# Eight block products against seven in one projection of a decoder layer, with the weights' sums made in DRAM by accumulating DMAs

## The chip, the core and the metric

The kernel runs on one core of one Trainium2 chip. A time is the device time of one execution in microseconds (us); the time of a kernel is the median of its runs.

## The reference

One decoder layer for 256 tokens of width 1024. `h @ w_in` feeds a pooling branch and an attention branch, `w_out` joins them, and a layer norm follows. Then comes the part that the change touches, cross-attention into 256 memory tokens, and after it a SwiGLU feed-forward and a last norm:

```python
def memory_cross_attention(h, mem, w_xq, w_xkv, w_xo):
    q = (h @ w_xq).reshape(B_, S_, XATTN_HEADS, XATTN_HEAD_DIM)
    kv = mem @ w_xkv
    k = kv[..., :D].reshape(B_, M, XATTN_HEADS, XATTN_HEAD_DIM)
    v = kv[..., D:].reshape(B_, M, XATTN_HEADS, XATTN_HEAD_DIM)
    ...
```

The memory's values are `mem @ w_xkv[:, D:]`: 256 x 1024 times 1024 x 1024, float32.

## The kernel before

**Precision.** Every float32 operand is split into a high part (ScalarE casts it to fp32r, L170, L429) and a low part (VectorE subtracts the high part, L172, L430). A product is three matmuls into one PSUM bank: high by high, high by low, low by high (`three`, L359 to L364).

**Weights.** `Stream` (L50 to L203) holds all weight tiles of 512 KB in the order in which they are used. `fetch` (L89) issues a tile's load on SyncE's queue (L102) into one of 7 raw buffers; `fetch_ahead` (L112) issues as many as the raw buffers allow, and `before` (L81) hangs other loads in front of a tile's. `prepare` (L148) makes the high and the low part of the next tile, in one of 8 buffers. A stage that reads weights through `get` (L181) lets one more tile be prepared at each call, until the stream is 8 tiles ahead of the last one that is used up; `next` (L176) does the same once for each tile that is used up. `held` stops both.

**Order.** The order on each engine is the order of the program's text (`manual_schedule`, L219): generators give out a few matmuls at a time (`run`, L420), and what stands between two calls of `run` stands between those matmuls in every queue. An engine goes through its queue strictly in that order.

**The stages that matter here**, in TensorE's order:

- `do_u` (L620): two halves; after each, VectorE adds `upad` (L627) and GpSimd computes the windows' sums (`windows`, L590: L596, L599).
- `do_xk` (L641), the memory's keys. Between its products stand `mix_pool` (L605 to L611), a matmul for each pooling group. Its input is made by `pool_diff` (L601 to L603) on VectorE from the windows' sums.
- `project(c_mix, ...)` and norm 1 (L784 to L790), which gives `h1`.
- `do_xv` (L796): the memory's values, 4 pieces (token half by column half) with 8 row blocks each, 3 matmuls of 512 columns for each: 96 matmuls. Each weight tile is one row block, 128 x 1024, and serves four pieces. After 8 steps, four groups of four transposes of `h1` (L440, `transpose_tok`) stand between its products; each takes a bank of the pool `pmisc`, which has four, and `split` reads it into `h1T`. At the end each piece is split into high and low from PSUM (L801).
- `do_xq` (L815): the queries of four heads. The first takes its two banks from `pmisc`, the others from `pacc`. `xscores(0)` (L828) follows after 7 steps of the second head and needs the first head's queries, which ScalarE (L822) and VectorE (L823, L825) take out of PSUM.

PSUM has eight banks: four in `pacc` (`accbank`), four in `pmisc` (`bank`).

Of the kernel before, what the change touches and what calls it, by code (L numbers as in the profile page):

```python
# [206 lines left out]
def decoder_layer(  # L207
    ctx: ExitStack, tc: tile.TileContext, x, x_t, mem_t, w_qkv, w_u, w_pool, w_out,
    ln1_g, ln1_b, w_xq, w_xk, w_xkv, w_xo, ln2_g, ln2_b, w_gu, w_down, ln3_g, ln3_b, out,
):  # L210
# [28 lines left out]
    def rows(w, k0, c0, nk=1, width=D):  # L239
        return ws.add(w[k0 * P:(k0 + nk) * P, c0:c0 + width].rearrange("(k p) n -> p k n", p=P), 1)  # L240
# [110 lines left out]

    mhalf = cp.tile([P, 32], F32, name="mhalf")[:, 0:1]
    nc.vector.memset(mhalf, -0.5)
# [81 lines left out]

    def transpose_tok(dst, tok, t, k0):

        ps = bank("tp")
        for k in range(4):
            nc.tensor.transpose(ps[:, k * P:(k + 1) * P], tok[:, (k0 + k) * P:(k0 + k + 1) * P], ident)  # L440
        ts = slice(t * P, (t + 1) * P)
        split(*dst.parts(k0, 4, ts), ps.rearrange("p (k t) -> p k t", k=4))
# [170 lines left out]
    def do_v():  # L613
# [3 lines left out]
        for piece in pieces:  # L617
            nc.scalar.copy(vt[:, piece[0], :], acc[piece])

    def do_u():  # L620
        for c in range(2):
            pss = [accbank("pu") for _ in range(2)]
            yield from proj_both(pss, c_u[c], xT, 4)
            for f, ps in enumerate(pss):
                y = upad[:, 2 * c + f, PADW:]
                nc.scalar.copy(y, ps[:, S:])
                nc.vector.tensor_add(y, ps[:, :S], y)  # L627
            windows(c)

    xkT = (a8("xkTh", F32R), a8("xkTl", F32R))  # L630
# [148 lines left out]


    load_norm("g", 1, ln1_g)()
    load_norm("b", 1, ln1_b)()
    h1 = ap.tile([P, T, D], F32, tag="a8", name="h1")
    mix = project(c_mix, lambda k: (cT[0][:, k], cT[1][:, k]), 4)  # L784
    for t in range(T):
# [10 lines left out]
    def do_xv():  # L796
        acc = {piece: accbank("xv") for piece in PIECES}
        yield from proj_rows(acc, c_xv, mT.pair,
                             PIECES, True, True, True)
        for t, c0, c1 in PIECES:  # L800
            split(xv[0][:, t, c0:c1], xv[1][:, t, c0:c1], acc[t, c0, c1])  # L801

    gv = do_xv()
    run(gv, 8)
    for t in range(T):
        for k0 in (0, 4):
            transpose_tok(h1T, h1[:, t, :], t, k0)
            run(gv, 2)
    run(gv)


# [323 lines left out]
    for half in HALVES:  # L1135
# [30 lines left out]
_INS = ["x", "x_t", "mem_t", "w_qkv", "w_u", "w_pool", "w_out", "ln1_g", "ln1_b", "w_xq", "w_xk",  # L1166
        "w_xkv", "w_xo", "ln2_g", "ln2_b", "w_gu", "w_down", "ln3_g", "ln3_b"]

# [43 lines left out]
```

## Time and profile before

| | us |
|---|---|
| median of 3 runs | 376.72 (376.57 to 377.14) |
| the profiled execution | 376.66 |
| its span in the trace | 374.9 |
| TensorE busy | 368.5 (98%) |
| VectorE busy | 306.8 (82%) |
| ScalarE busy | 204.1 (54%) |
| GpSimd busy | 19.6 (5%) |
| DMA, mean | 192 GB/s |

In the rows below, PE is TensorE, PEld its weight loads, DVE VectorE, ACT ScalarE, POOL GpSimd, SP SyncE. A row of a timeline has the start, the busy time, the engine and line, the operation, output and inputs, shapes, the count, and in brackets how long the engine was idle before and what ended that. A row of the table by stretches has the length of the stretch, the busy time of each engine in it, the clock that TensorE was granted, the share of the time that the 16 DMA engines were busy, and GB/s.

### The profile page before, as it was taken

How to read it: one execution, taken by the hardware profiler on the slowest of the kernel's cores; microseconds unless marked ns; L12 is line 12 of the kernel's file. 1: busy time of each engine (PE TensorE's matmuls, PEld its weight loads, DVE VectorE, ACT ScalarE, POOL GpSimd, SP SyncE). 2: the span in 40 equal slices, each digit the busy share in tenths (PEclk: the TensorE clock that was granted, in tenths of full speed). 3: DMA queues.
4: the chain of work that ended last, by engine and by line, in shares of the span. 5: the costliest groups of instructions: out<-in, count | busy, mean ns of one | idle time of the engine just before them, and what ended most of it. 6: DMA issues, size and time to landing. Idle time of an engine off the chain costs nothing.

```text
span 374.9 us, 5582 instructions
## 1 busy us (share of the span) xinstructions
PE 368.5 (98%) x2061; PEld 317.6 (85%) x2061; DVE 306.8 (82%) x498; ACT 204.1 (54%) x330; POOL 19.6 (5%) x27
## 2 busy tenths in 40 slices
PE   9999999999999999999999999999999999999994
PEld 8997878787888889998888888888898888888883
DVE  6768799975599677865889688888888999999984
ACT  6746677644154635644237675567665675546510
POOL 1000033400020000000100000000000000000021
PEclk9999999999999999999999999999999999999998
DMA  8997784668508963343106958665554453375202
GB/s 274 415 416 270 222 282 124 214 214 292 169 0 281 387 210 133 113 156 123 60 2 221 326 184 278 226 219 176 173 180 170 152 170 113 119 275 162 64 0 112
DMA packets 20891, 71.93 MB, mean 192 GB/s; under 512 B 2304, under 2 KB 3072, under 8 KB 20736
## 3 DMA queue, kind: packets, MB, share of 16 engines
q1 hardware_dynamic: 20432, 71.12, 54.3%
q10 hardware_dynamic: 432, 0.46, 0.4%
q8 instruction: 16, 0.26, 0.3%
q14 instruction: 11, 0.09, 0.1%
HBM read 70.52 MB, written 1.05 MB: 191 GB/s over the span
## 4 chain that ended last, share of the span: by engine, by line
PE 97%; DMA 1%; DVE 1%; ACT 0%; issue 0%; POOLq 0%; ACTq 0%
PE pg L377 19%; PE pg L383 10%; PE pqk L483 6%; PE m L362 5%; PE m L364 5%; PE m L363 5%; PE acc L362 4%; PE acc L363 4%; PE acc L364 4%; PE pxk L377 4%; PE pxq L377 4%; PE pxq L383 2%; PE pu L377 2%; PE pxk L383 2%; PE xv L362 2%; PE xv L364 2%
## 5 line engine op out<-in xcount | busy, mean ns | idle before, releaser
L725 POOL TENSOR_TENSOR rs<-rs,mhalf 128x1 f32<-128x1 f32 x6 | 5.0, 830 | 291.2 <-DVE rs L724 291.2
L429 ACT CAST g<-sg 128x512 fp32r<-128x512 f32 x14 | 8.7, 621 | 19.1 <-DVE sg L983 12.4
L430 DVE TENSOR_TENSOR g<-sg,g 128x512 fp32r<-128x512 f32 x14 | 9.7, 692 | 8.9 <-ACT g L429 8.9
L964 DVE TENSOR_TENSOR sg<-pg,sg 128x256 f32<-128x256 f32 x40 | 14.1, 416 | 0.0
L963 ACT COPY sg<-pg 128x256 f32<-128x256 f32 x40 | 11.8, 379 | 2.1 <-PE pg L383 2.1
L968 ACT ACTIVATE sg<-sg 128x512 f32<-128x512 f32 x10 | 6.3, 635 | 12.1 <-DVE sg L964 12.0
L520 ACT ACTIVATE xpr<-xs,mx 128x256 f32<-128x256 f32 x8 | 3.7, 470 | 14.3 <-DVE mx L531 14.3
L520 ACT ACTIVATE pr<-pr,mx 128x128 f32<-128x128 f32 (+1 forms) x16 | 7.1, 445 | 7.6 <-DVE mx L551 7.6
L429 ACT CAST h2T<-tp 128x512 fp32r<-128x512 f32 x4 | 2.3, 586 | 12.9 <-PE tp L440 12.9
L730 DVE SCALAR_TENSOR_TENSOR r<-r,mv,gb 128x512 f32<-128x512 f32 (+2 forms) x12 | 8.3, 722 | 0.0
L717 DVE BATCH_NORM_STATS2 st<-r 128x6 f32<-128x512 f32 (+1 forms) x12 | 8.0, 670 | 0.3
L969 DVE TENSOR_TENSOR sg<-sg 128x512 f32<-128x512 f32 x10 | 6.9, 692 | 0.8
L596 POOL TENSOR_TENSOR win<-upad 128x542 f32<-128x542 f32 x2 | 4.0, 1998 | 56.9 <-DVE upad L627 56.9
L525 DVE RECIPROCAL sm<-sm 128x2 f32<-128x2 f32 x12 | 2.0, 166 | 6.0 <-ACT xpr L520 4.5
L835 PE MATMUL xs<-xkTh,xq 128*128 128x256 f32 x32 | 6.4, 282 | 0.0
L429 ACT CAST h1T<-tp 128x512 fp32r<-128x512 f32 x4 | 2.4, 588 | 7.2 <-PE tp L440 7.2
L735 DVE SCALAR_TENSOR_TENSOR h<-r,rs,gb 128x512 f32<-128x512 f32 x8 | 5.7, 746 | 0.1
L596 POOL TENSOR_TENSOR win<-win 128x269 f32<-128x269 f32 (+3 forms) x4 | 5.8, 1446 | 0.2
L635 ACT CAST xkTh<-pxk 128x256 fp32r<-128x256 f32 x8 | 2.6, 377 | 5.5 <-PE pxk L383 5.5
L637 DVE TENSOR_TENSOR xkl<-pxk,xkTh 128x256 f32<-128x256 f32 x8 | 3.0, 416 | 3.1 <-ACT xkTh L635 3.1
L835 PEld LDWEIGHTS xs<-xkTh,xq 128*128 128x128 f32 x32 | 5.2, 190 | 0.2
L170 ACT CAST w39h<-w39r 128x1024 fp32r<-128x1024 f32 x1 | 1.0, 1049 | 7.8 <-PE acc L364 7.8
(1157 smaller groups left out, 1294.8 us busy)
## 6 DMA issues: line engine op xcount, KB each, us to landing
gb<-in_ln_g SPq DMA_DIRECT2D x3, 512.0 KB, 6.0
gb<-in_ln_b SPq DMA_DIRECT2D x3, 512.0 KB, 7.5
wr<-in_w_qkv SPq DMA_DIRECT2D x5, 256.0 KB, 4.4
mr<-in_mem_t SPq DMA_DIRECT2D x1, 1024.0 KB, 11.4
xt<-in_x SPq DMA_DIRECT2D x1, 1024.0 KB, 7.8
xr<-in_x_t SPq DMA_DIRECT2D x3, 256.0 KB, 6.1
wr<-in_w_qkv SPq DMA_DIRECT2D x1, 512.0 KB, 6.0
w7r<-in_w_qkv SPq DMA_DIRECT2D x1, 512.0 KB, 6.9
```

The lines of the kernel that those rows point to most:

```text
L362: nc.tensor.matmul(ps, wa, ya, start=start, stop=False, skip_group_check=part)
L363: nc.tensor.matmul(ps, wa, yb, start=False, stop=False, skip_group_check=part)
L364: nc.tensor.matmul(ps, wb, ya, start=False, stop=stop, skip_group_check=part)
L377: nc.tensor.matmul(ps, hi[:, b * P:(b + 1) * P], yT.both(k), start=k == 0, stop=False, skip_group_check=True)
L383: nc.tensor.matmul(ps[:, S:], lo[:, b * P:(b + 1) * P], yT.pair(k)[0], start=False, stop=k == KD - 1, skip_group_check=True)
L429: nc.scalar.copy(h, ps)
L483: nc.tensor.matmul(qk[i][:, f, :], w[:, c * P:(c + 1) * P], y, start=k == 0 and f == 0 and w is hi and y is x_hi, stop=k == KD - 1 and w i ...
L520: nc.scalar.activation(dst[:, j, :], src[:, j, :], AF.Exp, bias=mx[:, j:j + 1], scale=sign, accum_out=sm[:, j:j + 1])
L596: nc.gpsimd.tensor_add(nxt[:, j:, 2 * n - 1:], cur[:, j:, 2 * n - 1:], cur[:, j:, n - 1:PADW + S - n])
L835: nc.tensor.matmul(ps[:, t, :], q[:, kk, t * P:(t + 1) * P], k[:, 2 * h + kk], start=n == 0, stop=q is q_lo and kk == 1, skip_group_check= ...
L963: nc.scalar.copy(y[:, f, :], ps[:, S:])
L964: nc.vector.tensor_add(y[:, f, :], ps[:, :S], y[:, f, :])
```

## The change

The memory's values are computed by a form of Strassen's and Winograd's scheme: both factors are cut into quarters (the memory by token half and by even and odd row block, the weights by even and odd row block and by column half), and seven products of quarters, each over 4 row blocks, replace eight. `z` holds two sums of two quarters of the weights, `w` a sum of three and a sum of all four. They are made in DRAM: SyncE copies quarters of the weights into two DRAM tensors of 2 MB (`xv_z`, `xv_w`), and GpSimd issues three accumulating DMAs (`add_quarters`): 2 MB into `xv_z`, then 2 MB from `xv_z` into `xv_w`, then 1 MB into one half of `xv_w`. The first stands after the first `windows`, the second before the second `windows`, the third behind it. The stream then holds 14 tiles of 512 KB for the values in place of 8: 4 of `y` (two quarters as they are), 2 of `o`, 4 of `z`, 4 of `w`; each serves two steps of 3 matmuls, and `o` too. VectorE makes four sums of the memory's quarters and splits them. The seven products have seven banks, all four of `pmisc` and three of `pacc`; the four groups of transposes share the eighth, `tp`. `keep_xv` combines the seven into the four pieces.

```diff
-    c_xv = [rows(w_xkv, k, D) for k in range(KD)]
+    dram = ctx.enter_context(tc.tile_pool(name="dram", bufs=1, space=bass.MemoryType.DRAM))
+    xv_z, xv_w = [dram.tile([P, 2, KD // 2, 512], F32, name=name) for name in ("xv_z", "xv_w")]
+    c_xv = {("y", j): ws.add(w_xv[:, 0:2, j, :], 1)[0] for j in range(KD // 2)}
+    c_xv |= {("o", j): ws.add(w_xv[:, 3, j:j + 2, :], 1)[0] for j in range(0, KD // 2, 2)}
+    c_xv |= {("z", j): ws.add(xv_z[:, :, j, :], 1)[0] for j in range(KD // 2)}
+    c_xv |= {("w", j): ws.add(xv_w[:, :, j, :], 1)[0] for j in range(KD // 2)}
...
+    ws.before(c_xk[2][0], lambda: nc.sync.dma_start(xv_z, w_xv[:, 1:3]))
+    ws.before(c_xk[3][0], lambda: nc.sync.dma_start(xv_w, w_xv[:, 0:2]))
...
-    def transpose_tok(dst, tok, t, k0):
-
-        ps = bank("tp")
+    def transpose_tok(dst, tok, t, k0, ps=None):
+
+        ps = bank("tp") if ps is None else ps
...
+    def add_quarters(step):
+
+        if step == 0:
+            nc.gpsimd.dma_start(xv_z, w_xv[:, 2:4], accum_op=OP.add, max_dma_last_dim=8192)
+        elif step == 1:
+            nc.gpsimd.dma_start(xv_w, xv_z[:, 1:2].to_broadcast([P, 2, KD // 2, 512]), accum_op=OP.add, max_dma_last_dim=8192)
+        else:
+            nc.gpsimd.dma_start(xv_w[:, 0], w_xv[:, 1], accum_op=OP.add, max_dma_last_dim=8192)
+
     def do_u():
         for c in range(2):
...
+            if c:
+                add_quarters(1)
             windows(c)
+            add_quarters(2 if c else 0)
...
+    m_parts = [[late.tile([P, 2, KD // 2, P], F32R, tag=part, name=f"ms{i}{part}") for part in ("hi", "lo")]
+               for i in range(2)]
...
+    nc.vector.tensor_sub(s1, a21, a22)
+    nc.vector.tensor_sub(s3, a11, a21)
+    nc.vector.tensor_sub(s2, s1, a11)
+    nc.vector.tensor_add(s4, a12, s2)
+    for i, y in enumerate(sums):
+        hi, lo = m_parts[i // 2]
+        split(hi[:, i % 2], lo[:, i % 2], y)
...
     def do_xv():
-        acc = {piece: accbank("xv") for piece in PIECES}
-        yield from proj_rows(acc, c_xv, mT.pair,
-                             PIECES, True, True, True)
-        for t, c0, c1 in PIECES:
-            split(xv[0][:, t, c0:c1], xv[1][:, t, c0:c1], acc[t, c0, c1])
-
-    gv = do_xv()
-    run(gv, 8)
+        v = {n: bank(f"v{n}") for n in (2, 3, 7, 5)}
+        v |= {n: accbank(f"v{n}") for n in (1, 4, 6)}
+        plan = {"y": ((2, "12"), (3, "s4")), "z": ((7, "s3"), (5, "s1")), "w": ((4, "22"), (6, "s2")),
+                "o": ((1, "11"), (1, "11"))}
+        counts = dict.fromkeys(v, 0)
+        for (what, j), number in c_xv.items():
+            ws.prepare(number + 1)
+            hi, lo = ws.tiles[number]
+            for half, (n, form) in enumerate(plan[what]):
+                counts[n] += 1
+                three(v[n], memory(form, j + half if what == "o" else j), (hi[:, half], lo[:, half]),
+                      counts[n] == 1, counts[n] == KD // 2, True)
+                yield
+            ws.used += 1
+            ws.next()
+        return v
+
+    def keep_xv(v):
...
+        nc.scalar.copy(v1, v[1])
+        nc.vector.tensor_add(c11, v[2], v1)
+        nc.scalar.copy(v5, v[5])
+        nc.vector.tensor_add(c12, v[3], v5)
+        nc.vector.tensor_add(u2, v[6], v1)
+        nc.vector.tensor_add(c21, v[7], u2)
+        nc.vector.tensor_sub(c12, c12, u2)
+        nc.vector.tensor_sub(v5, v5, c21)
+        nc.vector.tensor_add(c21, v[4], c21)
+        for i, y in enumerate((c11, c12, c21, v5)):
+            split(quarter(0, *divmod(i, 2)), quarter(1, *divmod(i, 2)), y)
...
+    run(gv, 7)
+    tp = accbank("tp")
     for t in range(T):
         for k0 in (0, 4):
-            transpose_tok(h1T, h1[:, t, :], t, k0)
+            transpose_tok(h1T, h1[:, t, :], t, k0, tp)
             run(gv, 2)
     run(gv)
+    keep_xv(values[0])
```

The host lays the weights out as quarters (`w_xv`), without arithmetic on them, and the buffer for descriptors of GpSimd's DMAs grows (`dynamic_dma_scratch_size` 256 to 1024).

More of the change, by code (lines that the diff above doesn't have):

```diff
@@ L778, in until, with memory @@
                 return got
+    mix = project(c_mix, lambda k: (cT[0][:, k], cT[1][:, k]), 4)
+    run(mix, 2)
+    m_parts = [[late.tile([P, 2, KD // 2, P], F32R, tag=part, name=f"ms{i}{part}") for part in ("hi", "lo")]
+               for i in range(2)]
+    quarter = mr[0].rearrange("p (j e) (t s) -> p e t j s", e=2, t=T)
+    a11, a21, a12, a22 = [quarter[:, e, t] for e in range(2) for t in range(T)]
+    sums = [sp.tile([P, KD // 2, P], F32, name="ms", tag="pr", bufs=PR_BUFS) for _ in range(4)]
+    s1, s3, s2, s4 = sums
+    nc.vector.tensor_sub(s1, a21, a22)
[5 more added lines that the diff above has]
+        split(hi[:, i % 2], lo[:, i % 2], y)
+    def memory(form, j):
+        if form in ("11", "12", "22"):
+            e, t = {"11": (0, 0), "12": (1, 0), "22": (1, 1)}[form]
+            return mT.pair(2 * j + e, slice(t * P, (t + 1) * P))
+        i, n = divmod(("s1", "s3", "s2", "s4").index(form), 2)
+        return tuple(part[:, n, j] for part in m_parts[i])
     load_norm("g", 1, ln1_g)()
@@ L1201 @@
     given["w_xq"] = chunks(given["w_xq"])
+    quarters = given["w_xkv"][:, D:].reshape(KD // 2, 2, P, 2, 512)
+    given["w_xv"] = np.stack([quarters[:, i, :, j].transpose(1, 0, 2) for i, j in ((1, 0), (1, 1), (0, 1), (0, 0))],
+                             axis=1)
     given["w_gu"] = np.concatenate([chunks(given["w_gate"]), chunks(given["w_up"])], axis=3)
```

18 lines of the change are left out of this document (13 added, 5 removed).

## The prediction

> **What bounds the kernel now.** I read the page's busy times first, then the waits of TensorE alone, then stretches of 10 us around the stage, then single engines' timelines there.
>
> ```profile
> PE 368.5 (98%) x2061; PEld 317.6 (85%) x2061; DVE 306.8 (82%) x498; ACT 204.1 (54%) x330; POOL 19.6 (5%) x27
> ...
> PE end L1156 <- ACT diag L1153: 1.5, 1, 1.5
> PE busy L453 <- PEq L1175: 0.8, 1, 0.8
> PE acc L362 <- DVE xkTl L639: 0.2, 1, 0.2
> ...
> 30.00:40.00 10.00, 10.00 (x48) 7.78 (x48) 8.78 (x33) 7.99 (x21) 0.00 (x0) 1.00 0.49 180
> ...
> 50.00:60.00 10.00, 10.00 (x63) 8.24 (x62) 9.43 (x25) 8.00 (x19) 3.09 (x4) 1.00 0.45 152
> 60.00:70.00 10.00, 10.00 (x63) 8.34 (x61) 9.72 (x17) 5.80 (x10) 7.51 (x6) 1.00 0.73 221
> ...
> 90.00:100.00 10.00, 10.00 (x46) 8.29 (x45) 5.06 (x5) 3.14 (x3) 0.00 (x0) 1.00 0.63 218
> ...
> 110.00:120.00 10.00, 10.00 (x48) 8.26 (x47) 10.00 (x12) 4.08 (x5) 0.00 (x0) 1.00 0.59 197
> ```
>
> TensorE is the bound: three waits in the whole span, 2.5 us together, and full in every stretch quoted. So each matmul removed is worth its slot, and each wait put in front of TensorE is lost in full, since no idle time is left to take it up. The second thing to see is VectorE: in 110 to 120, in the middle of the stage that is changed, it is busy for 10.00 of 10.00 us. It is no bound there, because its weight tiles are ahead of need; but more work on it, or a wait of TensorE on work that stands late in its queue, is not hidden. I make the sum against the profiled execution, 376.66 us, which is 0.06 below the median of the runs.
>
> **The gain: 12 matmuls.** The values take 84 matmuls in place of 96 (seven products of 4 blocks of 3, for eight).
>
> ```profile
> 106.46 0.39 PE L362 MATMUL xv<-w35h,mT 128*128 128x512 f32 x1
> ...
> 130.20 1.98 PE L377 MATMUL pxq<-h1T,w43h 128*128 128x512 f32 x8
> ...
> 117.51 0.44 PE tp L440 x4
> ```
>
> From the first of the values' matmuls to the first of the queries' it is 23.74 us. Four groups of transposes lie in it, 0.44 each by the chain of work. (23.74 - 1.76) / 96 = 0.229 us for a slot; 12 slots are **-2.75 us**. A step of three takes 0.69.
>
> **First cost: GpSimd waits between its two windows.** The built program's queue on GpSimd reads: first windows, first accumulating DMA, second accumulating DMA, second windows. The second DMA reads what the first has written and so waits for its landing; the second windows stand behind that wait. An issuing queue does stand still at a DMA whose condition isn't met:
>
> ```profile
> SPq L102 <- DVE w63l L172: 17.8, 1, 17.8
> ...
> 55.43 0.28 POOL L599 TENSOR_TENSOR win<-win,fac 128x16 f32<-128x16 f32 x1
> 62.18 2.00 POOL L596 TENSOR_TENSOR win<-upad 128x542 f32<-128x542 f32 x1 [6.46 <-DVE upad L627]
> ...
> 68.83 0.22 POOL L599 TENSOR_TENSOR win<-win,fac 128x16 f32<-128x16 f32 x1
> ...
> 69.09 0.94 DVE L603 SCALAR_TENSOR_TENSOR upad<-win,upad 128x256 f32<-128x256 f32 x1 [0.28 <-POOL win L599]
> ...
> 70.17 0.67 PE L607 MATMUL pm<-upad,pool_w 128*128 128x256 f32 x2
> ```
>
> GpSimd is done with the first windows at 55.71 and starts the second at 62.18, so the transfer has 6.47 us. Behind it everything is tight: the third group's sum ends at 69.05, VectorE's difference waits for it and ends at 70.03, TensorE's pooling matmul starts at 70.17. A delay above some 0.2 us goes through to TensorE, and VectorE's next weight tile queues behind the same difference.
>
> No row shows an accumulating DMA, so its 2 MB (2.10 million bytes) are bounded by loads.
>
> ```profile
> GB/s 274 415 416 270 222 282 124 214 214 292 169 0 281 387 210 133 113 156 123 60 2 221 326 184 278 226 219 176 173 180 170 152 170 113 119 275 162 64 0 112
> ...
> w30r<-in_w_out SPq DMA_DIRECT2D x1, 512.0 KB, 3.4
> ```
>
> At the fullest slices the engines move 416 GB/s: 512 KB are 1.26 us of it, so 2.1 of the 3.4 us that such a load takes are fixed. One pass over 2.10 MB is 5.05, landing after 7.2 us. A transfer that reads two sources is two passes if reading sets the pace, 12.2 us; if the write counts as well, three, 17.3 us. I take two passes. The other loads hold the engines for 0.45 and 0.73 of 50 to 70, and the two copies of 2 MB that SyncE issues before two key tiles push some of 40 to 50 into it; fair sharing with them makes 12.2 into something between that and 25. I take 15, nearer the lower end, since the weight loads there are ahead of their use and come in bursts. Landing at 55.71 + 15 = 70.7, the second windows start 8.5 late, TensorE loses **+8.3 us** (bounds: 0.5 from one pass undisturbed, 20 from a crowded two passes; less than nothing is excluded, as a wait on a full TensorE gives nothing back).
>
> [...]
>
> **Second cost: one bank for four groups of transposes.** Before, each group had its own bank; now they share `tp`, which VectorE frees when it has subtracted (the low part of `h1T`).
>
> ```profile
> 111.35 1.22 DVE L172 TENSOR_TENSOR w39l<-w39r,w39h 128x1024 fp32r<-128x1024 f32 x1
> 112.49 1.22 DVE L172 TENSOR_TENSOR w40l<-w40r,w40h 128x1024 fp32r<-128x1024 f32 x1
> ...
> L430 DVE TENSOR_TENSOR h1T<-tp,h1T 128x512 fp32r<-128x512 f32 x4 | 2.8, 691 | 2.8 <-ACT h1T L429 2.8
> L429 ACT CAST h1T<-tp 128x512 fp32r<-128x512 f32 x4 | 2.4, 588 | 7.2 <-PE tp L440 7.2
> ```
>
> A weight tile's low part takes VectorE 1.14 from start to start. It comes out of norm 1 at 111.35, then by the built order makes tiles 39, 40, 41 and only then the first `h1T`: 111.35 + 3 x 1.14 + 0.69 = 115.45. TensorE has the first transposes at 106.46 + 7 x 0.69 = 111.3 and wants the bank again two steps later, at 113.1: 2.3 lost. From there each round is 0.44 + 1.37 on TensorE and 1.14 + 0.69 on VectorE, nearly equal, 0.3 more in the other two. **+2.6 us**; the values end at 130.3 (106.46 + 84 x 0.229 + 1.76 + 2.8 with small change), no earlier than before.
>
> **Third cost: the banks that the first queries need.** Four banks of `pmisc` hold products until `keep_xv`. The first queries take the first two, which VectorE frees with its first two sums, and these stand behind tiles 45 to 52. After the fourth `h1T` (121.4, three rounds of some 1.97 behind the first) eight tiles are 9.1 us: 130.7 with the little idle between. The two sums, 0.65 each (between 0.69 from PSUM, above, and 0.6 from SBUF, below), free the banks at 131.35 and 132.0; TensorE wants both from 130.3 on, the second one matmul later: **+1.5 us**.
>
> ```profile
> 130.34 2.48 DVE L430 TENSOR_TENSOR xv<-xv,xv 128x512 fp32r<-128x512 f32 x4
> ...
> 87.31 0.33 SPq L102 DMA_DIRECT2D w41r<-in_w_xkv  x1
> ```
>
> The first of these rows gives the 0.6 (2.48 / 4); the second is used below.
>
> **Fourth cost: the first scores.** The stream no longer stands 8 tiles ahead when the queries begin: `next` lets one tile follow for each used up, so depth stays at 4, where `get` filled it at the start of the stage. The rest is made up in the first queries: in the built order tiles 53 to 58 stand in front of the first queries' low parts, on VectorE and on ScalarE. Before, three tiles did, and it was done in time:
>
> ```profile
> 137.32 0.42 DVE L823 SCALAR_TENSOR_TENSOR xql<-pxq,xq 128x256 f32<-128x256 f32 x1
> ...
> 138.56 0.42 DVE L825 SCALAR_TENSOR_TENSOR xq<-pxq,xql 128x256 fp32r<-128x256 f32 x1
> ...
> 138.94 0.28 PE L835 MATMUL xs<-xkTh,xq 128*128 128x256 f32 x1
> ...
> 139.10 1.43 PE xs L835 x12
> ```
>
> After: `keep_xv` is 7 sums of 0.65 and 4 low parts of 0.6 from 130.7, so 137.6; six tiles, 144.4; the queries' low parts take 1.66 as before (137.32 to 138.98), 146.1. TensorE needs 8.74 from the first query matmul to the scores (130.20 to 138.94), so is there at 131.8 + 8.74 = 140.6; a third of the scores needs the low parts, 0.48 at the end. It ends at 146.6 and not at 140.6 + 1.43 = 142.0: **+4.6 us**. After that VectorE's order is the old one, six tile numbers on; 0.3 more at the second scores are left out.
>
> **Costed at nothing.** The four sums of the memory's quarters and their splits (5 us of VectorE) stand ahead of tile 35, in 87 to 98, where VectorE is busy for 5.06 of 10 us; without that cover they would be in front of norm 1, 1:1. The six more loads (3 MB) fall where DMA engines are idle or tiles are ahead. The `z` tiles wait on SyncE for the first transfer, with norm 1's scale and shift behind them in that queue, the `w` tiles for the third; before, the load in the place of the first `z` tile was issued at 87.31, and by the estimates the transfers have landed by then (70.7, then some 15 and 9 more with the windows between); at twice these times SyncE would stand and the load of `w` would be late, which is in the upper end.
>
> **Sum.** 376.66 - 2.75 + 8.3 + 2.6 + 1.5 + 4.6 = **390.9 us**. The last three terms (8.7) come from queue orders and durations that rows show; the first cost is the wide one.
>
> **Rivals.**
>
> - *The transfer is cheap.* One pass, little company: landing at 62.9 to 66, term 0.5 to 3.5, so 383.1 to 386.1. For it: 0.49 of the DMA's time is in use in 30 to 40 and loads alone land in 3.4. Against: two copies of 2 MB stand ahead in the same engines. 0.22.
> - *The transfer is crowded.* If copies in DRAM run at less than a load's rate, they still occupy the engines at 55.7, and the term passes 15: 397.6 and more. 0.20.
> - *Faster.* The place is VectorE's queue from 111 on, the price its three terms. If TensorE isn't held there, because the tiles' low parts come out sooner than by the sum (the handing back of `tp` needs them 2.3 us sooner, the scores 4.6), and the transfer lands inside its 6.47 us, 373.9 remains. It decides where all waits together stay under 2.75. Against: VectorE is full in 110 to 120 already. 0.06.
> - *The clock.* In the stretches quoted the granted clock is 1.00, and TensorE never waits for over 1.5 us, so no row shows what a wait of 8 us does to the matmuls behind it. If the next seven took twice their 0.229, 1.6 would be lost: 392.5. I give that 0.4 where the first term is over 3.4; it stays inside the ranges of those cases and is not in the sum. [...]
>
> That fewer matmuls aren't made is excluded: the built order holds 84.
>
> **How the numbers follow.** The forecast's case (term 3.5 to 15, 386.1 to 397.6) has 0.50, cheap 0.22, crowded 0.20, faster 0.06, no change 0.02. What a measurement of this kernel can tell from no change is about 0.2%, 0.75 us. The range takes in the cheap case with a third of VectorE's terms not coming (380) and the crowded case to a term of 20 (403); beyond it are the faster case and the worst of the crowded.
>
> **What would show it.** After, GpSimd's second windows start near 71 and not at 62; TensorE waits before the pooling matmul of the third group, before the second transposes of `h1`, before the first query matmuls, and before the last part of the first scores. Wrong would be: the second windows at 62 to 63 (first term gone), or a values' stage of 21 us with the scores straight after (the other terms gone).

## The result and the profile after

The changed kernel takes 399.25 us (median of five runs, 397.56 to 399.85); the kernel before took 376.76 us beside it. The ratio is 1.0585, 95% interval 1.0558 to 1.0611: slower by 22.5 us. The forecast was slower, at 390.9 us with a range of 380 to 403. The ratios here and below leave out an execution that lies more than 1.5% above the fastest of its kernel; there is one such in three of the kernels below (394.11, 391.88 and 384.94 us), and only their medians take it in.

The profiled execution took 399.48 us with a span of 397.7 (before: 376.66 and 374.9). From its page, the busy times, the row of the granted clock in 40 slices, and the two accumulating DMAs with the time from issue to landing at the end of the line:

```profile
PE 375.5 (94%) x2049; PEld 322.1 (81%) x2049; DVE 323.1 (81%) x519; ACT 212.9 (54%) x342; POOL 19.7 (5%) x30
...
PEclk9999999679999889699999999999999999999998
...
xv_z<-in_w_xv POOLq DMA_DIRECT2D x1, 2048.0 KB, 17.4
xv_w<-xv_z POOLq DMA_DIRECT2D x1, 2048.0 KB, 17.0
```

TensorE makes 12 matmuls fewer and is busy for 7 us longer. That alone says that part of the loss isn't waiting: the same matmuls take longer. The row of the clock says where: 6 and 7 in the eighth and ninth slice, 8, 8, 9 and 6 in slices 14 to 17. Before, every digit but the last was 9.

TensorE's waits (total, times, longest):

```profile
PE pm L614 <- DVE upad L610: 9.2, 1, 9.2
PE tp L447 <- DVE h1T L437: 2.1, 1, 2.1
PE xs L919 <- DVE xq L909: 1.8, 2, 1.6
PE pxq L384 <- ACT v L870: 1.6, 1, 1.6
...
PE xs L919 <- ACT xq L906: 0.7, 1, 0.7
PE pxq L384 <- DVE c L869: 0.4, 1, 0.4
```

These are the four places that the prediction names, and no other: the third pooling matmul, the second transposes, the first queries, the first scores. (Of the last, 0.7 us are ahead of the scores, for their high parts; the prediction has only the wait for the low parts.) GpSimd's timeline shows the first of them at its source (start, length, then in brackets the idle time and what ended it):

```profile
55.85 1.33 POOL L630 DMA_DIRECT2D xv_z<-in_w_xv  x1
73.62 1.07 POOL L632 DMA_DIRECT2D xv_w<-xv_z  x1 [16.43 <-DMA xv_z<-in_w_xv]
74.23 1.57 POOL L603 TENSOR_TENSOR win<-upad 128x542 f32<-128x542 f32 x1
...
90.90 0.87 POOL L634 DMA_DIRECT2D xv_w<-in_w_xv  x1 [11.44 <-DMA xv_w<-xv_z]
```

The second windows begin at 74.23 and not at 62.18, behind the wait of the second DMA for the first.

Stretches of 2 us (the columns: length, then busy time and count of each engine, the granted clock, the share of the DMA engines, GB/s) show what follows each stop:

```profile
80.00:82.00 2.00, 2.00 (x9) 1.82 (x8) 1.61 (x4) 0.47 (x1) 0.00 (x0) 0.50 1.10 236
...
84.00:86.00 2.00, 2.00 (x14) 1.24 (x13) 2.00 (x3) 0.97 (x2) 0.00 (x0) 1.00 1.01 227
...
124.00:126.00 2.00, 0.67 (x3) 0.24 (x2) 2.00 (x2) 0.71 (x1) 0.00 (x0) 1.00 0.32 92
126.00:128.00 2.00, 1.19 (x7) 1.07 (x8) 1.89 (x3) 0.49 (x2) 0.00 (x0) 1.00 0.94 273
128.00:130.00 2.00, 2.00 (x9) 1.54 (x7) 1.62 (x2) 1.04 (x2) 0.00 (x0) 0.54 0.93 313
130.00:132.00 2.00, 2.00 (x7) 1.62 (x7) 1.18 (x3) 1.54 (x2) 0.00 (x0) 0.61 0.95 368
...
162.00:164.00 2.00, 2.00 (x11) 2.00 (x11) 0.88 (x4) 2.00 (x6) 0.00 (x0) 0.50 0.60 244
```

Behind the stop of 9.2 us TensorE is full again from 80 on, but at half clock; at 84 it is back. The stop of 2.1 us before 126.81 is followed, after 1.2 us at full clock, by some 3.4 us near half clock. The same comes back behind 144, and behind the first scores, where stops of 0.7, 1.6 and 0.2 us follow each other, for about twice as long (from 159 to about 165.7).

Where the span grew, by the starts of TensorE's first matmuls of each kind (us from the span's start):

| first matmul of | before | after | gap grown by |
|---|---|---|---|
| the values | 106.46 | 117.78 | 11.32 |
| the queries | 130.20 | 144.56 | 3.04 |
| the scores | 138.94 | 156.43 | 3.13 |
| the transposed probabilities | 144.13 | 166.80 | 5.18 |
| the gates | 188.53 | 211.19 | -0.01 |

All of the 22.7 us lies between 70 and 167 us. TensorE's waits listed above add up to 15.8; less the 2.75 of the matmuls that is 13.1. Some 9.6 us are left that no wait shows.

### The profile page after: what moved, and what is told of

Same layout as the page of the kernel before. It is cut to its first block, busy times and chain, and to the rows that moved or that the text cites. A ratio compares the mean times of both kernels' runs of the same rounds, so it can differ in the third digit from the quotient of the medians.

```text
span 397.7 us, 5627 instructions
## 1 busy us (share of the span) xinstructions
PE 375.5 (94%) x2049; PEld 322.1 (81%) x2049; DVE 323.1 (81%) x519; ACT 212.9 (54%) x342; POOL 19.7 (5%) x30
## 4 chain that ended last, share of the span: by engine, by line
PE 60%; DVE 5%; ACT 2%; DMA 2%; issue 1%; POOLq 0%; ACTq 0%; DVEq 0%
PE pg L384 18%; PE pg L390 10%; PE m L369 4%; PE m L371 4%; PE m L370 4%; PE pxq L384 2%; PE acc L369 2%; PE acc L370 2%; PE acc L371 2%; PE pxq L390 2%; DMA w52r<-in_w_xq 2%; PE xs L919 1%; PE pg L371 1%; PE tp L447 1%; PE pg L369 1%
## 5 line engine op out<-in xcount | busy, mean ns | idle before, releaser
L614 PE MATMUL pm<-upad,pool_w 128*128 128x256 f32 x8 | 3.1, 473 | 9.2 <-DVE upad L610 9.2
L919 PE MATMUL xs<-xkTh,xq 128*128 128x256 f32 x32 | 7.5, 313 | 2.5 <-DVE xq L909 1.8
L610 DVE SCALAR_TENSOR_TENSOR upad<-win,upad 128x256 f32<-128x256 f32 x4 | 2.1, 542 | 9.0 <-POOL win L606 9.0
L614 PEld LDWEIGHTS pm<-upad,pool_w 128*128 128x128 f32 x8 | 1.4, 221 | 9.6 <-issue 9.6
L447 PE MATMUL tp<-ident,h 128*128 128x128 f32 x32 | 5.3, 292 | 2.1 <-DVE h1T L437 2.1
L447 PEld LDWEIGHTS tp<-ident,h 128*128 128x128 f32 x32 | 4.2, 150 | 3.7 <-DVE h1T L437 2.8
## 6 DMA issues: line engine op xcount, KB each, us to landing
xv_z<-in_w_xv POOLq DMA_DIRECT2D x1, 2048.0 KB, 17.4
```

The lines of the kernel that those rows point to most:

```text
L919: nc.tensor.matmul(ps[:, t, :], q[:, kk, t * P:(t + 1) * P], k[:, 2 * h + kk], start=n == 0, stop=q is q_lo and kk == 1, skip_group_check= ...
```

## The experiments

The diffs are excerpts; lines with + are added to the changed kernel, or to the kernel that the text names. Each ratio is to the kernel before on the same chip.

### The second accumulating DMA behind the second windows

```diff
-            if c:
-                add_quarters(1)
             windows(c)
-            add_quarters(2 if c else 0)
+            if c:
+                add_quarters(1)
+                add_quarters(2)
+            else:
+                add_quarters(0)
```

> The second accumulating DMA is issued behind the second windows, everything else as in the changed kernel. If the wait of GpSimd between its windows is the first cost, the second windows start at 62 to 63 again, TensorE's 9.2 us wait before the third pooling matmul goes, and the slow matmuls behind it with it (2.0): 399.2 - 11.3 = 387.9 us, with the values' stage and the first scores unchanged. Rival, the loads: TensorE waits in the same place for weight tiles that the added transfers hold up (ScalarE waited 5.2 us for tile 28, until 73); then a wait of some us stays between 70 and 90 and the time is 390 or more.

392.8 us, ratio 1.0422 (1.0393 to 1.0451). GpSimd's second windows, TensorE's new wait, the time from issue to landing of norm 1's gain and shift, then the low part and the load of `w34` and SyncE's queue:

```profile
62.88 1.99 POOL L603 TENSOR_TENSOR win<-upad 128x542 f32<-128x542 f32 x1 [5.27 <-DVE upad L643]
...
118.20 0.50 PE L370 MATMUL v<-w39l,mT 128*128 128x512 f32 x1 [4.49 <-DVE w39l L172]
...
DMA to landing us min/median/max: 17.3/17.6/17.9
...
L172 DVE TENSOR_TENSOR w34l<-w34r,w34h x1: 1226/1226/1226, 89.2 to 89.2; 128x1024 fp32r<-128x1024 f32 x1
...
w34r<-in_w_out SPq DMA_DIRECT2D x1, 512.0 KB, 19.6
...
90.50 0.62 SPq L102 DMA_DIRECT2D w41r<-xv_z  x1
91.17 0.59 SPq L332 DMA_DIRECT2D gb<-in_ln_g  x1
```

The windows are back at 62.88 and the stop of 9.2 us at the pooling is gone, so the prediction's first cause is shown. But the time is 4.9 us above what was expected, and 4.5 us of the stop came back elsewhere. Norm 1's gain is issued at 91.17 (83.41 before), right behind `w41r`, and lands some 17 us later; VectorE waits 4.5 us for it, and TensorE 4.5 us for a low part that VectorE makes behind the norm. What held `w41r` was not `z`, which had landed at 73.8 (56.29 + 17.5): it was issued 0.1 us after VectorE had made `w34l` (89.2 + 1.2) and with that freed a buffer, and `w34` itself came 19.6 us after its issue. The loads among the copies and accumulating DMAs (`w25` to `w34`) take 14 to 21 us here. Besides, the wait for the high parts at the first scores is 2.2 us (0.7 in the changed kernel).

### TensorE kept busy through the first stop

```diff
     attend(2)
+    keep_busy(34)
     mix_pool(2)
```

> 34 matmuls of zeros, 128 columns each, that nobody reads, stand in front of the third pooling matmul, so TensorE is at work in most of its 9.2 us wait. If the slow matmuls after the wait come from the clock that drops in an idle stretch, the clock stays at 1.00 there and the time falls by 2.0 to some 397.2 us. Rival, the memory traffic slows them (the DMA engines are full at that time): the matmuls after the wait stay slow and the time stays at 399.2 or rises by what the fillers overrun.

396.81 us, ratio 1.0533 (1.051 to 1.0556). TensorE's timeline:

```profile
70.20 7.86 PE L460 MATMUL busy<-const-float32-0.0 128*128 128x128 f32 x68
79.37 0.70 PE L614 MATMUL pm<-upad,pool_w 128*128 128x256 f32 x2 [1.31 <-DVE upad L610]
79.72 1.30 PE L390 MATMUL pxk<-mT,w22l 128*128 128x256 f32 x8
```

The pooling matmul starts at the same time as before the filler (79.53 in the trace after), so the wait is as long; but the eight matmuls behind it take 1.30 us, and in the changed kernel they took 2.27. The edit leaves the transfers as they are, and the mean granted clock is 0.987 (0.966 in the changed kernel). So it is the clock and not the traffic: 2.4 us for this one stop by the medians, 2.0 by the ratios.

### The chain of DMAs alone, on the kernel before

The kernel before, with its 96 matmuls, gets the two copies and the three accumulating DMAs at the places that the change has them, on other rows of the weights; nobody reads what they make. Of the edit, the part on GpSimd:

```diff
+            if c:
+                add_quarters(1)
             windows(c)
+            add_quarters(2 if c else 0)
```

> The kernel before with its 96 matmuls, and added to it only the two copies of 2 MB and the three accumulating DMAs at the places of the changed kernel, on other rows of the weights; nobody reads the sums. If the chain of transfers is a cost by itself and of the size that the trace shows, 376.7 + 9.4 + 2.0 = 388.1 us, with the second windows at 74. Rival, the six more weight loads and the reads of the sums share in it: the first accumulating DMA lands sooner than in 17.4 us and the time is under 386.

389.44 us, ratio 1.0325 (1.0305 to 1.0345), with the one wait

```profile
PE pm L614 <- DVE upad L610: 9.8, 1, 9.8
```

So the chain costs 12.7 us by itself: the stop of 9.8, and 2.9 for the clock (mean 0.984) and what was not taken apart. The rival is out: without the six more weight loads the stop is no shorter than the 9.2 us of the changed kernel, and the time is not under 386.

### One accumulating DMA where it is quiet

The kernel before, with one accumulating DMA of 2 MB issued at 104.9 us, behind norm 1, and one plain copy of 2 MB by GpSimd at 186 us.

> The kernel before, with one accumulating DMA of 2 MB in DRAM issued behind the first power of norm 1 (about 103 us, where the DMA engines move 33 GB/s) and one plain copy of 2 MB in DRAM from the same queue behind the first power of norm 2 (about 184 us). They are read by nobody. One pass: landing after 7.2 us; two passes 12.2; three passes 17.3, which would leave nothing for company in the 17.4 us of the changed kernel. The plain copy: 7.2 if DRAM to DRAM goes at a load's rate, about 12 if at half of it. Time 376.7 in every case, since nothing waits for them.

377.75 us in one run. The issues, with the time to landing:

```profile
xv_z<-in_w_xkv POOLq DMA_DIRECT2D x1, 2048.0 KB, 13.1
xv_w<-in_w_xkv POOLq DMA_DIRECT2D x1, 2048.0 KB, 8.9
```

13.1 us is nearest to the estimate of two passes (12.2; one was 7.2, three 17.3). It isn't wholly undisturbed: from 113.4 us on, weight loads are issued beside it, while the copy at 186 us has no company (the kernel before moves 0 to 3 GB/s from 186 to 196). And the plain copy, at 8.9, is itself 1.7 us above one pass as the prediction priced it. The ratio of the accumulating DMA to the copy is 1.47 here, where the estimates of two passes and of one (12.2 and 7.2) have 1.69. In the changed kernel's place the same transfer took 17.4, so the heavier company there costs some 4.3 us more.

### Norm 1's gain and shift ahead of the accumulated tiles

On top of the first experiment:

```diff
-    load_norm("g", 1, ln1_g)()
-    load_norm("b", 1, ln1_b)()
+    ws.before(c_xv["z", 0], load_norm("g", 1, ln1_g))
+    ws.before(c_xv["z", 0], load_norm("b", 1, ln1_b))
```

> The kernel with the second accumulating DMA behind the windows (392.8 us), and the first norm's gain and bias now loaded ahead of the first load of z, not behind it. Theory (SP's queue gives the cost back: gain and bias stood behind a load that waited for the accumulated z, landed 17.6 us after issue, VectorE waited 4.5 us and TensorE 4.5 us on w39's low part): that wait goes, and with it the low clock behind it, some 1.7 us: 392.8 - 6.2 = 386.6 us. Rival (VectorE is late by itself in that stretch, or another load takes the place of the gain's): the wait stays with another releaser and the time is 391 us or more.

(That the load ahead of the gain waited for `z`, as this says, is wrong by the row of `w34l` above; the gain's place behind it is right.)

389.51 us, ratio 1.0333 (1.03 to 1.0367). The wait on `w39l` falls from 4.5 to 0.7 us, as expected; the time falls by 3.3 us (by the ratios 3.4), half of what was expected. The profiled executions lie 5.2 us apart (394.02 and 388.80), and the runs of either kernel are spread over some 3 us, so the gain is known only to within 2 us or so. What the edit doesn't touch are the waits at the first scores, 2.2 us for the high parts as in the first experiment, and 1.9 for the low ones. In the stretch from 140 to 150:

```profile
PE xs L921 <- ACT xq L908: 2.2, 1, 2.2
...
140.00:150.00 10.00, 6.20 (x37) 5.08 (x36) 9.97 (x13) 7.26 (x10) 0.00 (x0) 1.00 0.90 309
```

VectorE (the third busy time) is full there, and from 103 to 150 us its longest idle time is 1.1. TensorE, busy for 6.20 of the 10 us, waits for it.

### No sums of the weights at all

All fourteen tiles are read straight from the input; there are no copies, no accumulating DMAs and no waits for them. What is left out are the sums of the quarters of the weights, so the values that it computes are of other weights.

```diff
-    c_xv |= {("z", j): ws.add(xv_z[:, :, j, :], 1)[0] for j in range(KD // 2)}
-    c_xv |= {("w", j): ws.add(xv_w[:, :, j, :], 1)[0] for j in range(KD // 2)}
+    c_xv |= {("z", j): ws.add(w_xv[:, 1:3, j, :], 1)[0] for j in range(KD // 2)}
+    c_xv |= {("w", j): ws.add(w_xv[:, 0:2, j, :], 1)[0] for j in range(KD // 2)}
```

> The changed kernel without the sums of the weights: all fourteen tiles are read straight from the input, so there are no copies in DRAM, no accumulating DMAs and no waits for them (left out: the sums, so the values are of other weights). The seven products, their banks and VectorE's sums stay. Theory (the DMAs cost by the waits that they place on GpSimd and SP, not by their traffic): the wait of 9.2 us and its clock go, the other waits stay: before 376.7 - 2.75 for the matmuls + 11.3 that the trace of after shows between the values' first matmul and the first gates beyond the matmuls' gain (3.0 + 3.1 + 5.2, the 2.75 being in them already), so 376.7 + 11.4 = 388.1 us at most, and 386.6 as in the kernel with the gain loaded early. Rival (three passes of 2 MB in a crowded stretch slow the other loads): 4 us or more below that kernel. Second rival (seven products are free without the sums): 374 us.

386.74 us, ratio 1.0253 (1.0238 to 1.0268): 9.6 us above before. With the 12.7 us of the chain alone that makes 22.3, and the change costs 22.5. So the loss has two halves that add up: the chain of DMAs, and what the seven products bring without it (more tiles and sums for VectorE, one bank for the transposes, the clock behind their stops), net of the 12 matmuls. It is 2.8 us below the kernel with the early gain, so by this comparison the crowding that is left there costs less than the rival's 4.

### TensorE kept busy in all four stops

```diff
     attend(2)
+    keep_busy(34)
     mix_pool(2)
...
+            if t == 0 and k0 == 4:
+                fill(held[2], 8)
             transpose_tok(h1T, h1[:, t, :], t, k0, tp)
...
+    fill(tp, 6)
     run(xq[0])
```

`fill` adds matmuls of zeros into a bank that is open or free; two and six more stand around the high parts of the first scores.

> The changed kernel with TensorE kept busy in all four of its new waits: 34 matmuls on zeros ahead of the third pooling matmul, 8 ahead of the second group of transposes, 6 ahead of the first queries, 2 and 6 around the first scores' high parts. No wait is shorter; only the clock is told apart. With the first filler alone it took 396.8 us. Theory (the clock halves for some 3.4 us behind every stop of TensorE, of 2 us as of 9): the three later stretches at half clock go too, some 1.7 us each: 396.8 - 5 = 391.8 us, mean clock 0.99. Rival (stops of 2 us do not lower the clock; the slow matmuls there have another cause): 396.8 us, with the clock at 0.5 in the same places.

394.14 us, ratio 1.0442 (1.0425 to 1.0459), mean clock 0.999 (0.966 in the changed kernel). The fillers and what is still waited for behind them:

```profile
123.03 1.95 PE L466 MATMUL v<-const-float32-0.0 128*128 128x128 f32 x16
125.33 0.66 PE L447 MATMUL tp<-ident,h 128*128 128x128 f32 x4 [0.35 <-DVE h1T L437]
...
140.20 1.50 PE L466 MATMUL tp<-const-float32-0.0 128*128 128x128 f32 x12
142.07 0.50 PE L384 MATMUL pxq<-h1T,w49h 128*128 128x512 f32 x1 [0.37 <-ACT v L878]
143.05 1.86 PE L384 MATMUL pxq<-h1T,w49h 128*128 128x512 f32 x7 [0.48 <-DVE c L877]
...
153.94 0.39 PE L933 MATMUL xs<-xkTh,xq 128*128 128x256 f32 x1 [1.65 <-ACT xq L916]
155.02 1.50 PE L466 MATMUL tp<-const-float32-0.0 128*128 128x128 f32 x12
156.82 0.39 PE L933 MATMUL xs<-xkTh,xq 128*128 128x256 f32 x1 [0.30 <-DVE xq L919]
```

The clock stays up in all four places, so in the changed kernel the stops lowered it (to 0.50 to 0.61), those of some 2 us too. By the ratios the clock is worth 5.4 us in all (1.0585 to 1.0442), 2.0 of it at the first stop. That is 3.4 us for the three later ones, where 5 was expected: from the first query to the first scores TensorE takes 11.87 us with the clock at half and 11.87 with it up, since it only arrives earlier and waits longer for VectorE.

### Banks, early sums and a hold, together

On top of the kernel with the early gain: three banks for the four groups of transposes; `v1`, `c11`, `v5` and `c12` made inside `do_xv` as soon as their products are done; and

```diff
+    ws.held = True
     run(xq[0])
     run(xq[1], 7)
     xscores(0)
+    ws.held = False
```

> The kernel with the second accumulation behind the windows and gain and bias loaded early, and besides: three banks for the transposes in place of one, the first two sums of the products (two copies, two additions) made as soon as their products are done rather than behind the preparation of ten tiles, and the preparation of tiles held while the first queries' parts are made. Theory (the rest of the loss is waits that the order of VectorE's work makes, with the clock behind each): the waits of 2.1, 2.0 and 2.5 us go with their clock: 386.6 - 10 = 376 to 378 us, and 374 if nothing is left of them. Rival (VectorE is full in that stretch, so that what is moved ahead makes something else late): a wait of like size on a tile's low part, 383 us or more.

389.39 us, ratio 1.0282 (1.0217 to 1.0348); the runs lie from 384.7 to 394.1. TensorE's waits:

```profile
PE xs L929 <- ACT xq L916: 2.9, 1, 2.9
PE v L372 <- DVE w39l L172: 2.2, 1, 2.2
PE xs L929 <- DVE xq L919: 1.8, 3, 1.2
```

The rival holds. Of the rows, the first and the third are at the second scores; the second, for the low part of `w39`, is back at 2.2 us (0.7 in the kernel with the early gain); VectorE waits 1.1 us for norm 1's shift ahead of it, and the rest was not taken apart. The stop at the transposes is gone, the first scores start 8.7 us behind the first queries as they did before the change; but the eight tiles that were held are then prepared at once, ahead of the second queries' parts, and the same stop is found at the second scores (at 155 and 158 us, and 0.4 us of the third row at the first).

### VectorE relieved by GpSimd

On top of the kernel with the early gain, every third low part of tiles 41 to 62 goes to GpSimd, six of them ahead of the first scores; and the same with three banks and early sums.

```diff
-                (eng or nc.vector).tensor_sub(lo[:, :, s], raw[:, :, s], r32(hi[:, :, s]))
+                aside = 41 <= i <= 62 and i % 3 == 2
+                (nc.gpsimd if aside else eng or nc.vector).tensor_sub(lo[:, :, s], raw[:, :, s], r32(hi[:, :, s]))
```

> The kernel with the second accumulation behind the windows and gain and bias loaded early (389.5 us), with one change: the low parts of every third tile from 41 to 62 are subtracted by GpSimd, which is idle there, not by VectorE. Theory (VectorE is the bound from norm 1 to the first scores: six more tiles at 1.14 us and seven sums at 0.6 to 0.7 us, 11.4 us, stand ahead of the first queries' low parts in its queue, and it was busy without a gap from 103 to 150 us): six of its subtractions before the first scores leave it, 6.8 us; first scores come 5 to 6 us earlier, the clock stays up, and the time is 382 to 384 us. Rival (TensorE's waits there come from the banks and the order, not from VectorE's load): 388.5 us or more. Second rival (GpSimd, 1.30 us for 128x512 in the trace of before, hence 2.6 us a tile, is itself late for the tiles): new waits of TensorE for a low part from GpSimd, 388 us or more.

> The same with three banks for the transposes and the first two sums made as soon as their products are done, without the hold on the tiles. Theory: of the waits that the relief leaves, those for the transposes' low part (2.1 us) and for the first queries' banks (0.7 us) go with their clock: 2 to 4 us below the run above, 379 to 381 us, so still above before (377.1 us), since the matmuls' 2.75 us stand against the first scores' softmax latency and the crowded transfers. Rival (with VectorE relieved these two had gone already): the same time as the run above within 1 us. To beat before it would have to come below 376 us.

395.3 us, ratio 1.0488 (1.0459 to 1.0516), and 395.54 us, ratio 1.0514 (1.0461 to 1.0567): 5.8 and 6.0 us slower than the kernel with the early gain (389.5), where 382 to 384 and 379 to 381 us were expected. From the first of the two, GpSimd's and VectorE's timelines:

```profile
144.65 2.47 POOL L173 TENSOR_TENSOR w53l<-w53r,w53h 128x1024 fp32r<-128x1024 f32 x1 [10.00 <-ACT w53h L170]
147.49 2.95 POOL L173 TENSOR_TENSOR w56l<-w56r,w56h 128x1024 fp32r<-128x1024 f32 x1 [0.37 <-ACT w56h L170]
...
145.55 2.65 DVE L173 TENSOR_TENSOR w54l<-w54r,w54h 128x1024 fp32r<-128x1024 f32 x1 [0.70 <-ACT w54h L170]
148.13 3.40 DVE L173 TENSOR_TENSOR w55l<-w55r,w55h 128x1024 fp32r<-128x1024 f32 x1
151.45 1.21 DVE L173 TENSOR_TENSOR w57l<-w57r,w57h 128x1024 fp32r<-128x1024 f32 x1
```

A tile's low part takes VectorE 1.21 us, but 2.65 and 3.40 where GpSimd makes one at the same time, and each of these ends 1.1 us behind the end of GpSimd's (147.12 and 148.20; 150.44 and 151.53). So in these rows VectorE got no further until GpSimd was done; what held it, they don't show. The relief took six tiles (6.8 us) off VectorE ahead of the first scores, and what VectorE did beside them took some 10 us longer. It says nothing against VectorE as the bound: with VectorE slower the kernel became slower.

### Tiles prepared at the pace of their use

On top of the kernel with banks and early sums: gain and shift two tiles earlier still (in front of `c_xv["o", 0]`), and in place of the hold

```diff
+    ws.held = True
     run(xq[0])
+    ws.prepare(c_xq[2][0] + 1)
     run(xq[1], 7)
     xscores(0)
+    ws.prepare(c_xq[2][0] + 2)
     run(xq[1])
+    ws.prepare(c_xq[3][0] + 1)
     run(xq[2], 3)
```

and so on, two tiles a head, with the release before `run(xq[3])`.

> The kernel with the second accumulation behind the windows, three banks for the transposes and the first two sums made early, as in the fourth kernel of the second group (389.4 us), with two edits: gain and bias are loaded two tiles earlier still, and tiles are prepared two for each head of the queries from the first queries on (one behind the first queries' parts, one behind the first scores, and so on), neither six ahead of them nor eight at once behind the first scores. GpSimd subtracts nothing. Theory (VectorE holds the path from norm 1 to the second scores: 6 tiles, 6.8 us, stand in its queue ahead of what TensorE waits for, while it is idle for 10.7 us from 150 to 190 us in the trace of before): the waits on the queries' parts, 2.9 + 1.8 us in the fourth kernel of the second group, go with their clock, and that on w39's low part, 2.2 us, shrinks to 1 us: 389.4 - 4.7 - 1.2 - 3 to 5 for the clock = 378.5 to 380.5 us. Rival (the work is only put off: the same tiles are late at the second or the third queries, or at the output's products): a wait of 3 us or more for a tile's part behind the first scores, 385 us or more. To beat before it would have to come below 376 us.

384.68 us, ratio 1.0197 (1.0164 to 1.0231). One new wait is left, and VectorE's timeline has its cause:

```profile
PE acc L371 <- DVE xq L919: 5.2, 1, 5.2
...
165.23 1.22 DVE L172 TENSOR_TENSOR w64l<-w64r,w64h 128x1024 fp32r<-128x1024 f32 x1
166.37 0.41 DVE L917 SCALAR_TENSOR_TENSOR xql<-pxq,xq 128x256 f32<-128x256 f32 x1
```

Until the third scores TensorE is now level with the kernel before (the first head's values begin at 154.9 us, before at 155.3). Then the release puts `w59` to `w64` ahead of the last head's low part, once more the same stop. The forecast of 378.5 to 380.5 us missed that one; it is what the rival says, a wait of over 3 us further on, though at the last head and not where the rival looked.

### The pace kept to the end

```diff
-    ws.held = False
+    ws.prepare(c_xo[0][0] + 2)
     run(xq[3])
+    ws.held = False
```

and `w52` is prepared between the sums of the products and their splits.

> The paced kernel (384.7 us) with two edits: the pace is kept to the end of the last head's queries (there the release put six tiles, w59 to w64, on VectorE ahead of their low part, and TensorE waited 5.2 us), and w52 is prepared behind the sums of the products rather than ahead of them. Theory (in the paced kernel TensorE reached the first head's values at 154.9 us, before at 155.3; only that last burst of VectorE stands between it and before): the 5.2 us go with some 1.7 us of the clock, and 0.5 of the 0.9 us at the scores: 384.7 - 7.4 = 377.3, between 376 and 378.5 us, the same as before (377.1) within 0.4%, since of the matmuls' 2.75 us all but 0.4 are gone by the first scores' transposes. Rival (the six tiles are only put off once more, to norm 2 and the last products of that stage, where VectorE has 9 us idle for their 6.8): a wait of 2 us or more for VectorE between 165 and 195 us, 380 us or more.

377.29 us against 376.81, ratio 1.0012 (0.9989 to 1.0035): the same as before within what can be told. TensorE's busy time, and its waits beside the two at the kernel's start and end that before has too:

```profile
PE 367.4 (98%) x2049; PEld 316.5 (85%) x2049; DVE 322.1 (86%) x519; ACT 213.1 (57%) x342; POOL 22.9 (6%) x30
...
PE xs L931 <- DVE xq L921: 0.4, 1, 0.4
PE acc L371 <- DVE xkTl L662: 0.2, 1, 0.2
```

The whole 22 us is found again, with all five DMAs and all seven products in place; but the 12 matmuls that are gone still gain nothing that can be told. From the first of the values' matmuls to the first of the queries' it now takes 21.33 us (before 23.74), which is 2.4 of the 2.75 us. By the gates 0.8 us of it is left. The kernel starts the second windows 0.9 later, and takes 0.7 longer between the first scores and their transposes. The times fall into two groups, six runs near 375.9 and five near 378.8 us; the profiled one (376.06) is of the lower. What parts the groups was not found.

## Why the prediction was right, and by how much it was short

**The number.** The measured time, 399.25, lies above the forecast's own case (386.1 to 397.6) and in the part of the range that was laid out for a crowded transfer with a first term over 15. The first term was 9.2. So the place in the range is in part luck: room kept for one cause was filled by another, the clock.

**The four stops.** They came where the sum put them, and without the clock in play they have about the size that it gave them. In the kernel with the fillers, where filler and wait together are the stop, they are 9.2, 2.3, 2.4 and 4.4 us, some 18.2 in all; the sum had 8.3, 2.6, 1.5 and 4.6, 17.0. In the changed kernel itself the last reads 2.5, since TensorE comes late with its clock down.

**The first term** was only 0.9 short, but two errors stand against each other in it. The second windows started 12.05 us late (74.23 and not 62.18), where the sum had 8.5: the landing was taken as 15 us and was 17.4 (two passes undisturbed were taken as 12.2, a choice that no row of before showed, and one such DMA took 13.1 in the quieter place), and the second DMA's own issue stands ahead of the windows, from 73.62. That this goes through in full, as nothing behind it has slack, was wrong. The third group's sum ended only 9.4 us late (78.41 and not 69.05), as GpSimd's middle two additions were faster (first row before, second after):

```profile
64.26 4.49 POOL L596 TENSOR_TENSOR win<-win 128x538 f32<-128x538 f32 x2
...
75.88 2.23 POOL L603 TENSOR_TENSOR win<-win 128x538 f32<-128x538 f32 x2
```

Before, VectorE works beside them; after, it stands idle for 9.0 us behind the same stop. They take 4.49 us in the trace with the second DMA moved too, where that stop is gone. So 2.7 us of the delay came back, and the nearness of 8.3 to 9.2 is luck.

**The third term** was 0.5 short of the 2.0 measured after. In the changed kernel ScalarE waited 2.5 us for the load of `w52`, and VectorE with it 1.2 us ahead of the sums. That load was issued at 135.58, right behind VectorE's work on `w45` (135.55), seven tiles before it, which freed a raw buffer, and took 6.8 us to land. The sum let VectorE go through the eight tiles with little idle between and put no load among them. Whether the six more loads, costed at nothing, made this one slow wasn't tried alone.

**The clock is the step that failed.** It was left out of the sum as a rival of 1.6 us at one place, tied to a first term over 3.4. It took part behind every stop, those of 2.1 us and of 1.6 and 0.4 too, and cost 5.4 us by the ratios. No run shows a bound at 3.4 us, and no row of before the factor of two. After, it was near half (0.54 and 0.61 in the two stretches from 128 to 132) for some 3.4 us behind the stop of 2.1 us too (124.67 to 126.81).

**What is left** of the 8.4 us that the sum fell short of the median: 5.4 clock, 1.2 in the stops, and some 1.8 that was not taken apart; 0.2 of it is there ahead of the first stop (the first pooling matmul starts at 62.23 and not at 62.05).

**Costed at nothing, and hidden only by the first cost.** That norm 1's gain stands in SyncE's queue behind the first load of `z` cost nothing in the changed kernel, because everything else was 9 us late. It cost 4.5 us as soon as the stop on GpSimd was gone. The working named the queue and the loads behind it, but looked for the cost in the landing of `z`. It lay in the crowd: weight loads that took 14 to 21 us in place of the 3.4 of the row quoted, and a buffer that came free late.

**The reason behind terms two to four.** The prediction treats them as three places in VectorE's queue. The last two kernels show that they are one thing: 14 tiles of 512 KB in place of 8 bring six low parts (6.8 us) and seven sums (4.6) into a stretch in which VectorE was full from 110 to 120 and busy for 21.0 of the 30 us behind that, and the look-ahead of the weight queue puts them in front of what TensorE needs next. Prepared at the pace of their use they fit, in the 10.7 us that VectorE idles between 150 and 190 in the kernel before. These kernels also have three banks, early sums and an earlier gain, and the earlier gain and the pace came in together, so what each of these is worth by itself isn't shown.

## What to carry to other kernels

Where TensorE was full, as here (98% busy), a wait was lost in full and some of the clock behind it, so the 12 matmuls (2.75 us) were worth less than one stop of 2.1 us with its slow stretch (some 1.7 us more, half of 3.4): price each new wait with some 1 to 2 us on top (2.0 at the first stop here, 3.4 at the three others). When an edit trades matmuls for vector work, the place of that work in the queue matters more than its amount; a look-ahead counted in tiles grows with the number of tiles, and must be told again how far to run. And when a stop is removed, look at once at what was late behind its cover: here the load of a gain vector in another queue gave half of it back.

## What the runs showed of the hardware

- In the changed kernel a stop of TensorE of 2.1 us was followed by some 3.4 us at a granted clock of 0.5 to 0.6, after about 1.2 us at full clock; behind stops of 0.7, 1.6 and 0.2 us close together it was some 6.7 us. With matmuls on zeros in the gaps the mean granted clock was 0.999, without them 0.966.
- An accumulating DMA of 2 MB from DRAM to DRAM landed 13.1 us after its issue on GpSimd's queue in a stretch with few loads, 17.4 among copies and many loads (the changed kernel); a plain copy with no company took 8.9. Each issue held GpSimd for 0.9 to 1.3 us in the changed kernel.
- Loads of 512 KB (`w25` to `w34`) landed 14 to 21 us after issue while copies and accumulating DMAs of 2 MB ran (with the second DMA moved; up to 22.7 in the changed kernel), 3.3 to 8.3 in the kernel before.
- With every third low part on GpSimd, VectorE's subtraction of a tile (1.21 us by itself) took 2.65 and 3.40 us beside one of GpSimd's and ended 1.1 us behind it; GpSimd took 2.4 to 3.4 us for a tile. Two additions of windows took GpSimd 4.49 us beside a working VectorE (before) and 2.23 beside an idle one (after).
